# Norm sums of a hybrid encoder layer by 512-column products with constant matrices

## The chip, the core and the metric

The kernel runs on one core of a Trainium2 chip. TensorE (PE) multiplies, VectorE (DVE) and ScalarE (ACT) work elementwise, GpSimd (POOL) fills a few constants, and SyncE (SP) issues the DMAs. Each engine has its own queue of instructions. The metric is the time of one execution on the device, in microseconds; smaller is better.

## The reference, cut to what matters

One layer of a streaming encoder over 256 tokens, width 2048. A modulated norm feeds one input projection; three token mixers (stick-breaking attention, retention, differential attention) work on its columns; their results are gated, merged and projected; a gated MLP with a short convolution follows. The change touches three norms inside the mixers:

```python
def rms_norm(x, g):
    y = x * rsqrt(mean(x * x, axis=-1) + EPS)
    return y * g

# differential attention: 4 heads, each with 2 maps of 64 columns
dq = rope(rms_norm(d_q.reshape(B, S, 4, 2, 64), diff_qn))
dk = rope(rms_norm(d_k.reshape(B, S, 4, 2, 64), diff_kn))
y_diff = differential_attention(dq, dk, d_v, lam)            # heads of 128
y_diff = rms_norm(y_diff, diff_on) * (1.0 - lam_init)

# retention: 4 heads of 256 columns
mu = mean(y, axis=-1); var = mean((y - mu) ** 2, axis=-1)
y_ret = (y - mu) * rsqrt(var + EPS) * g + b                  # then * silu(r_g)
```

## The kernel before, in words

Activations lie with the feature on the partition and the token in the column: `P` = 128 partitions, `S` = 256 tokens. Weights stream from memory in chunks of 128x1024 floats (`raw`). Each chunk is split in two: ACT casts it to a shorter format (`hi`, line 145), DVE subtracts that from the raw one (`lo`, line 118), and PE takes `hi` against a 512-column pair and `lo` against 256 columns (line 349); eight such pairs make one chunk's work. There are 7 buffers for `raw`, 6 for `hi` and 4 for `lo`, so DVE can be at most four chunks ahead of PE. Between chunks DVE also folds the modulation weights (`raw<-raw,c_b`, line 121, one 128x1024 pass each; "modulation pass" below).

The mixers are written as jobs that lie between the units of the gate and branch products: `unit_T` does one unit (four chunks for a gate, one or more for a branch), the list `order` runs through 24 of them, and `jobs` says which job comes before which unit. A scheduler then orders each engine's instructions from priorities and its own estimate of the times, so a job's instructions end up among the products of neighbouring units.

A norm of the mixers is made so: ACT squares, PE sums over partitions with the squares as weights and a column of ones (or `blk`, two columns for the two halves) as the moving operand (`rstd_rows`, line 237). That gives the sum with the token on the partition, 1 to 32 columns wide. DVE makes 1/rms of it by an integer first guess and three Newton steps on these few columns (`small`). To use it, it must go back to token-in-column on all partitions: a column is broadcast to 128 and transposed by PE with `ident` (`spread`, line 253). `diff_prep` does it for q and k of the differential heads at once (for k through a 256-column copy, line 608; the q part stays a per-token scale `qsc`), `diff_pair` for two heads' results, `ret_pair` for two retention heads (`ret_mid` makes their products, lines 706 and 707, copies at 709 and squares at 711). In `diff_head` PE transposes the probabilities at line 645 after DVE has made them. `ret_out` finishes the retention heads: for each head DVE takes a 512-column product with `sum_a`, two with `prm` and two that make the `x` tiles.

ACT's queue also holds ACT_TABLE_LOADs, seven before the change; one of them stands ahead of the first gate's Tanh (line 760).

## Time and profile before

| what | value |
|---|---|
| median of 3 runs | 1528.62 us (1525.99 to 1530.25) |
| profiled execution | 1530.01 us |
| span of its instructions | 1528.2 us |
| PE busy | 1516.9 us (99%) |
| DVE busy | 1251.1 us (82%) |
| ACT busy | 803.0 us (53%) |
| granted clock of PE, mean | 0.999 |
| chain that ended last | PE 91%, DVE 5%, DMA 2%, ACT 1% |

The first row is the metric. The span runs from the first to the last instruction of one profiled execution, and 1.8 us of its time lie outside. Busy shares are of the whole span; matmuls overlap, so a busy PE isn't PE at its peak. The chain is followed back from the last instruction, at each step to what released it.

### The profile page before, as it was taken

How to read it: one execution, taken by the hardware profiler on the slowest of the kernel's cores; microseconds unless marked ns; L12 is line 12 of the kernel's file. 1: busy time of each engine (PE TensorE's matmuls, PEld its weight loads, DVE VectorE, ACT ScalarE, POOL GpSimd, SP SyncE). 2: the span in 40 equal slices, each digit the busy share in tenths (PEclk: the TensorE clock that was granted, in tenths of full speed). 3: DMA queues.
4: the chain of work that ended last, by engine and by line, in shares of the span. 5: the costliest groups of instructions: out<-in, count | busy, mean ns of one | idle time of the engine just before them, and what ended most of it. 6: DMA issues, size and time to landing. Idle time of an engine off the chain costs nothing.

```text
span 1528.2 us, 24447 instructions
## 1 busy us (share of the span) xinstructions
PE 1516.9 (99%) x9228; PEld 1347.0 (88%) x9228; DVE 1251.1 (82%) x2062; ACT 803.0 (53%) x1202; POOL 1.6 (0%) x10
## 2 busy tenths in 40 slices
PE   8999999999999999999999999999999999999999
PEld 7899898988889998888899888888888888888888
DVE  6899889789989899988989877656777776677765
ACT  7534335455654455455557656544565543455541
POOL 0000000000000000000000000000000000000000
PEclk9999999999999999999999999999999999999999
DMA  9988896668799859898966777776777776666672
GB/s 353 327 345 342 308 333 232 198 204 290 257 310 319 328 197 355 310 316 309 321 203 217 234 215 230 226 230 219 226 230 219 224 231 190 187 189 187 187 210 78
DMA packets 108374, 385.38 MB, mean 252 GB/s; under 512 B 12384, under 2 KB 14048, under 8 KB 108256
## 3 DMA queue, kind: packets, MB, share of 16 engines
q1 hardware_dynamic: 108112, 383.75, 76.1%
q8 instruction: 72, 1.18, 0.3%
q14 instruction: 46, 0.38, 0.1%
q10 hardware_dynamic: 144, 0.08, 0.0%
HBM read 379.58 MB, written 2.10 MB: 250 GB/s over the span
## 4 chain that ended last, share of the span: by engine, by line
PE 91%; DVE 5%; DMA 2%; ACT 1%; issue 1%; SPq 0%; ACTq 0%; DVEq 0%
PE acc L349 46%; PE mps L349 26%; PE acc L419 2%; PE acc L418 2%; PE acc L417 2%; DVE lo L118 2%; DVE raw L121 1%; PE acc L431 1%; PE acc L430 1%; PE acc L429 1%; PE mps L417 1%; PE mps L419 1%; PE mps L418 1%; DMA raw<-in_ada 1%; PE mps L430 1%
## 5 line engine op out<-in xcount | busy, mean ns | idle before, releaser
L145 ACT CAST hi<-raw 128x1024 fp32r<-128x1024 f32 x520 | 543.3, 1051 | 436.1 <-PE acc L349 139.0
L118 DVE TENSOR_TENSOR lo<-raw,hi 128x1024 fp32r<-128x1024 f32 x520 | 632.8, 1221 | 145.6 <-PE acc L349 62.6
L349 PE MATMUL acc<-h,hi 128*128 128x512 f32 (+1 forms) x1116 | 392.4, 393 | 0.0
L349 PE MATMUL acc<-h,lo 128*128 128x256 f32 x1104 | 299.4, 281 | 0.0
L121 DVE SCALAR_TENSOR_TENSOR raw<-raw,c_b 128x1024 f32<-128x1024 f32 x192 | 232.0, 1221 | 39.9 <-DMA raw<-in_ada 39.5
L349 PEld LDWEIGHTS acc<-h,hi 128*128 128x128 f32 x1116 | 207.4, 189 | 40.9
L349 PE MATMUL acc<-b,hi 128*128 128x512 f32 x640 | 230.6, 394 | 0.0
L349 PE MATMUL mps<-b,hi 128*128 128x512 f32 x640 | 230.0, 394 | 0.0
L349 PEld LDWEIGHTS acc<-h,lo 128*128 128x128 f32 x1104 | 209.1, 189 | 7.1 <-issue 1.3
L349 PE MATMUL acc<-b,lo 128*128 128x256 f32 x640 | 173.1, 281 | 0.0
L349 PE MATMUL mps<-b,lo 128*128 128x256 f32 x640 | 173.0, 281 | 0.0
L349 PEld LDWEIGHTS acc<-b,hi 128*128 128x128 f32 x640 | 118.9, 188 | 25.0
L349 PEld LDWEIGHTS mps<-b,hi 128*128 128x128 f32 x640 | 118.7, 188 | 25.0
L349 PE MATMUL mps<-h,hi 128*128 128x512 f32 (+1 forms) x380 | 131.7, 387 | 0.0
L349 PEld LDWEIGHTS mps<-b,lo 128*128 128x128 f32 x640 | 120.6, 188 | 3.3
L349 PEld LDWEIGHTS acc<-b,lo 128*128 128x128 f32 x640 | 120.6, 188 | 3.3
L349 PE MATMUL mps<-h,lo 128*128 128x256 f32 x368 | 99.1, 280 | 0.0
L349 PE MATMUL acc<-a,hi 128*128 128x512 f32 (+1 forms) x320 | 91.7, 349 | 0.0
L417 PE MATMUL acc<-h,hi 128*128 128x256 f32 x304 | 83.6, 281 | 1.8 <-ACT h L311 1.8
L418 PE MATMUL acc<-h,hi 128*128 128x256 f32 x304 | 84.8, 281 | 0.0
L419 PE MATMUL acc<-h,lo 128*128 128x256 f32 x304 | 84.2, 283 | 0.3 <-DVE lo L118 0.2
L121 DVE SCALAR_TENSOR_TENSOR tmp<-ftmp,prm,tmp 128x255 f32<-128x255 f32 (+1 forms) x160 | 76.6, 479 | 7.5 <-ACT tmp L883 7.5
(254 smaller groups left out, 2259.9 us busy)
## 6 DMA issues: line engine op xcount, KB each, us to landing
raw<-in_ada SPq DMA_DIRECT2D x192, 512.0 KB, 5.2
raw<-in_wu SPq DMA_DIRECT2D x176, 512.0 KB, 4.3
raw<-in_wg SPq DMA_DIRECT2D x96, 512.0 KB, 4.9
raw<-in_wd SPq DMA_DIRECT2D x88, 512.0 KB, 4.1
raw<-in_w0b SPq DMA_DIRECT2D x32, 512.0 KB, 5.7
raw<-in_w0c SPq DMA_DIRECT2D x32, 512.0 KB, 6.1
raw<-in_w0a SPq DMA_DIRECT2D x32, 512.0 KB, 5.6
raw<-in_wb SPq DMA_DIRECT2D x32, 512.0 KB, 5.4
```

The costliest lines, as they stand in the source:

```text
L118: V.tensor_tensor(out, a, b, op=op)
L121: return V.scalar_tensor_tensor(out, a, s, b, op0=op0, op1=op1, **kw)
L145: return r, hi, SC.copy(hi, r)
L349: PE.matmul(*x, start=first and k == 0, stop=last and k == len(m) - 1)
L417: PE.matmul(dst, wh, hT[kt][:, 0:S], start=(kt == k0 and g % 2 == 0), stop=False)
L418: PE.matmul(dst, wh, hT[kt][:, S:2 * S], start=False, stop=False)
L419: PE.matmul(dst, wl, hT[kt][:, 0:S], start=False, stop=(kt == k1 and g % 2 == 1))
L429: PE.matmul(dst, hh, wh, start=(kt == k0), stop=False)
L430: PE.matmul(dst, hl, wh, start=False, stop=False)
L431: PE.matmul(dst, hh, wl, start=False, stop=(kt == k1))
```

## The change

k of the differential heads, their results and the retention heads get their 1/rms from a new function, `rstd_wide`. PE takes a constant matrix of ones as weights (or `halves`, two 64x64 blocks of ones) and the squares as the moving operand, so that every partition gets the sum with the token in the column. On 512 columns (two heads, or one tile of k) ACT takes logarithm, a scaled copy and exponential, and DVE three steps. The transposes, the broadcasts and the 256-column copies go; q keeps `rstd_rows`, now 16 columns wide.

```diff
-    def spread(cols):
...
+    def rstd_wide(mask, xs_, scale):
+        ss = mps()
+        n = 512 // len(xs_)
+        for k, x in enumerate(xs_):
+            PE.matmul(ss[:, k * n:(k + 1) * n], mask, x, start=True, stop=True)
+        r, v, q = wk(), wk(), wk()
+        SC.activation(r, ss, AF.Ln, bias=eps, scale=scale)
+        SC.activation(r, r, AF.Exp, scale=-0.5)
+        SC.activation(v, ss, AF.Identity, bias=eps, scale=scale)
+        stt(q, v, -0.5, r)
+        tt(q, q, r, ALU.mult)
+        stt(r, q, 1.5, r, op0=ALU.add)
+        return r
...
+    halves = keep.tile([P, P], F32, name="halves")
+    nc.gpsimd.memset(halves, 0.0)
+    for j in range(0, P, 64):
+        nc.gpsimd.memset(halves[j:j + 64, j:j + 64], 1.0)
...
     def diff_prep():
...
-            jobs += [[sq[:, 0:S]], [sq[:, S:2 * S]]]
+            if len(jobs) < 4:
+                jobs += [[sq[:, 0:S]], [sq[:, S:2 * S]]]
+            else:
+                ks.append(sq)
         y = rstd_rows(jobs, blk, 1.0 / 64.0)
         ts_(qsc, y[:, 0:16], 0.125)
+        rk = [rstd_wide(halves, [sq], 1.0 / 64.0) for sq in ks]
...
-            for j in range(2 if k >= 2 else 0):
-                o = 4 * (2 * k + j)
-                e = tmp()
-                V.tensor_copy(e.rearrange("p (a b) -> p a b", b=64),
-                              y[:, o:o + 4].unsqueeze(2).to_broadcast([P, 4, 64]))
-                r = spread([e[:, 0:P], e[:, P:S]])
-                tt(x[:, j * S:(j + 1) * S], x[:, j * S:(j + 1) * S], r, ALU.mult)
+            if k >= 2:
+                tt(x, x, rk[k - 2], ALU.mult)
...
     def diff_pair(h):
...
-        c = rstd_rows(jobs, ones[:, 0:1], 1.0 / 128.0)
+        r = rstd_wide(ones, jobs, 1.0 / 128.0)
         for k, yn in enumerate(yns):
-            r = spread([c[:, 2 * k + b:2 * k + b + 1].to_broadcast([P, P]) for b in range(2)])
-            stt(yn, yn, lamc[:, 1:2], r)
+            stt(yn, yn, lamc[:, 1:2], r[:, k * S:(k + 1) * S])
...
     def ret_pair(h0):
-        jobs = [ret_mid(h0), ret_mid(h0 + 1)]
-        c = rstd_rows(jobs, ones[:, 0:1], 1.0 / 256.0)
+        both_r = rstd_wide(ones, [ret_mid(h0), ret_mid(h0 + 1)], 1.0 / 256.0)
         for k in range(2):
...
-            r = spread([c[:, 2 * k + b:2 * k + b + 1].to_broadcast([P, P]) for b in range(2)])
+            r = both_r[:, k * S:(k + 1) * S]
```

Three places show how the instructions move. The first is ACT's queue at the retention heads. Before, the copies and squares of two heads (lines 709, 711), two casts, and the next two heads:

```order
L709 COPY a_5744<-mps_5739 128x512
L711 ACTIVATE a_5746<-mps_5739 128x512
L709 COPY a_5754<-mps_5749 128x512
L711 ACTIVATE a_5756<-mps_5749 128x512
L145 CAST hi_6015<-raw_6013 128x1024
L145 CAST hi_6040<-raw_6038 128x1024
L709 COPY a_5794<-mps_5789 128x512
L711 ACTIVATE a_5796<-mps_5789 128x512
L709 COPY a_5804<-mps_5799 128x512
L711 ACTIVATE a_5806<-mps_5799 128x512
```

Now (the lines of the copies and squares are 720 and 722; 257, 259 and 258 are logarithm, scaled copy and exponential):

```order
L722 ACTIVATE a_5724<-mps_5717 128x512
L257 ACT_TABLE_LOAD
L257 ACTIVATE a_5730<-mps_5727,eps 128x512
L259 ACTIVATE a_5731<-mps_5727,eps 128x512
L258 ACT_TABLE_LOAD
L258 ACTIVATE a_5730<-a_5730 128x512
L720 COPY a_5748<-mps_5743 128x512
L722 ACTIVATE a_5750<-mps_5743 128x512
L720 COPY a_5758<-mps_5753 128x512
L722 ACTIVATE a_5760<-mps_5753 128x512
L145 CAST hi_5955<-raw_5953 128x1024
L145 CAST hi_5980<-raw_5978 128x1024
```

The five instructions of a pair, two of them table loads, stand ahead of the next two heads' copies and of both casts. The same five, for the second pair, follow these casts. The same two loads stand in each of the six calls of `rstd_wide`, twelve in all.

The second place is DVE's queue from the modulation passes after the retention products on. Before, the few-column steps (`small`) stand among passes and splits:

```order
L118 TENSOR_TENSOR a_5756<-a_5756 128x256
L127 TENSOR_SCALAR small_5764<-mps_5759 128x4
L121 SCALAR_TENSOR_TENSOR raw_6044,part<-raw_6044,c_b 128x1024
L125 TENSOR_SCALAR small_5765<-small_5764 128x4
L118 TENSOR_TENSOR lo_5954<-raw_5950,hi_5952 128x1024
L127 TENSOR_SCALAR small_5765<-small_5765 128x4
L118 TENSOR_TENSOR small_5766<-small_5765 128x4
```

Now:

```order
L121 SCALAR_TENSOR_TENSOR raw_5984,part<-raw_5984,c_b 128x1024
L121 SCALAR_TENSOR_TENSOR a_5732<-a_5731,a_5730 128x512
L118 TENSOR_TENSOR lo_5894<-raw_5890,hi_5892 128x1024
L118 TENSOR_TENSOR a_5732<-a_5732,a_5730 128x512
L118 TENSOR_TENSOR a_5750<-a_5750 128x256
L121 SCALAR_TENSOR_TENSOR a_5730<-a_5732,a_5730 128x512
L118 TENSOR_TENSOR a_5760<-a_5760 128x256
L121 SCALAR_TENSOR_TENSOR a_5712<-a_5712,prm,a_5730 128x256 x2
L121 SCALAR_TENSOR_TENSOR a_5722<-a_5722,prm,a_5730 128x256 x2
L118 TENSOR_TENSOR lo_5935<-raw_5931,hi_5933 128x1024
L121 SCALAR_TENSOR_TENSOR a_5768<-a_5767,a_5766 128x512
L118 TENSOR_TENSOR lo_5957<-raw_5953,hi_5955 128x1024
```

The second row reads `a_5730`, which is ACT's exponential of the first pair, and stands ahead of a split `lo` of the weights; the last row but one reads that of the second pair, again with splits behind it.

The third place is DVE's queue at the end of `ret_out`. Before, up to the two splits there:

```order
L118 TENSOR_TENSOR ftmp_6089<-acc_5989,ftmp_6089 128x256
L121 SCALAR_TENSOR_TENSOR x_6159<-a_6156,x_6159 128x256
L121 SCALAR_TENSOR_TENSOR a_6166<-a_5804,prm,a_6166 128x256 x2
L118 TENSOR_TENSOR ftmp_6094<-acc_5990,ftmp_6094 128x256
L118 TENSOR_TENSOR lo_6182<-raw_6178,hi_6180 128x1024
L121 SCALAR_TENSOR_TENSOR ftmp_6130<-gate_5938,acc_6098 128x256
L121 SCALAR_TENSOR_TENSOR x_6169<-a_6166,x_6169 128x256
L118 TENSOR_TENSOR b_4773<-b_4773,ftmp_6130 128x256
L121 SCALAR_TENSOR_TENSOR ftmp_6133<-gate_5943,acc_6099 128x256
```

Now:

```order
L118 TENSOR_TENSOR ftmp_6034<-acc_5930,ftmp_6034 128x256
L121 SCALAR_TENSOR_TENSOR x_6099<-a_6096,x_6099 128x256 x2
L121 SCALAR_TENSOR_TENSOR ftmp_6070<-gate_5878,acc_6038 128x256
L121 SCALAR_TENSOR_TENSOR a_6106<-a_5758,prm,a_6106 128x256
L118 TENSOR_TENSOR b_4741<-b_4741,ftmp_6070 128x256
L121 SCALAR_TENSOR_TENSOR a_6106<-a_5758,prm,a_6106 128x256
L121 SCALAR_TENSOR_TENSOR ftmp_6073<-gate_5883,acc_6039 128x256
L121 SCALAR_TENSOR_TENSOR x_6109<-a_6106,x_6109 128x256
L118 TENSOR_TENSOR b_4741<-b_4741,ftmp_6073 128x256
L121 SCALAR_TENSOR_TENSOR x_6109<-a_6106,x_6109 128x256
L118 TENSOR_TENSOR lo_6122<-raw_6118,hi_6120 128x1024
```

`lo_6122` is the split that was `lo_6182`. Two gate products (`ftmp<-gate`), two sums (`b`) and two `x` steps that stood behind it stand ahead of it now. Between the split before it (`lo_6104` before, `lo_6044` now) and this one lie now 26 instructions: 4 of 512 columns, 8 with `prm`, 8 of `x`, 2 of `ftmp<-acc`, 2 gate products and 2 sums.

## Rows read from the trace of the kernel before

**Rows 1.** Page, part 1: engine, busy us, share of the span, instructions.

```profile
PE 1516.9 (99%) x9228; PEld 1347.0 (88%) x9228; DVE 1251.1 (82%) x2062; ACT 803.0 (53%) x1202; POOL 1.6 (0%) x10
```

**Rows 2.** Busy by stretch: from:to us, length, engines' busy (instructions), granted clock, DMA.

```profile
316.80:320.30 3.50, 3.50 (x33) 3.46 (x32) 1.42 (x4) 3.23 (x6) 0.00 (x0) 1.00 1.01 394
321.80:325.00 3.20, 3.20 (x12) 2.71 (x11) 3.20 (x7) 0.53 (x1) 0.00 (x0) 0.50 0.25 22
340.00:410.00 70.00, 68.91 (x407) 58.72 (x406) 66.27 (x150) 43.37 (x91) 0.00 (x0) 1.00 0.76 259
...
517.00:557.00 40.00, 39.92 (x258) 35.99 (x257) 36.05 (x90) 22.02 (x39) 0.00 (x0) 1.00 0.57 186
```

**Rows 3.** Timeline of PE at diff_prep: start us, length us, instruction, xcount.

```profile
316.85 3.63 PE L237 MATMUL mps<-x,a 128*128 128x2 f32 x32
320.34 0.49 PE L349 MATMUL acc<-h,hi 128*128 128x512 f32 x1
...
335.47 1.04 PE L253 MATMUL mps<-x,tmp 128*128 128x128 f32 x8
336.27 0.48 PE L349 MATMUL acc<-a,lo 128*128 128x256 f32 x2
```

**Rows 4.** Timeline of PE at the retention heads.

```profile
522.85 0.48 PE L349 MATMUL acc<-h,hi 128*128 128x512 f32 x1
...
524.22 0.50 PE L237 MATMUL mps<-ones,a 128*128 128x1 f32 x4
524.58 0.37 PE L349 MATMUL acc<-h,lo 128*128 128x256 f32 x1
...
532.09 0.62 PE L253 MATMUL mps<-x,small 128*128 128x128 f32 x4
532.54 0.60 PE L706 MATMUL mps<-a,a 128*128 128x256 f32 x2
532.98 0.39 PE L707 MATMUL mps<-a,a 128*128 128x128 f32 x2
```

**Rows 5.** What PE waited for, 300 to 560 us: us in total, times, longest.

```profile
PE mps L645 <- DVE a L121: 0.9, 2, 0.7
```

**Rows 6.** Timeline of PE: transposes of the second differential head's probabilities, brackets: idle before.

```profile
366.21 0.30 PE L645 MATMUL mps<-x,a 128*128 128x128 f32 x1 [0.25 <-DVE a L121]
```

**Rows 7.** Timeline of ACT: a table load, and a 512-column square of retention.

```profile
317.44 1.28 ACT L760 ACT_TABLE_LOAD   x1
318.73 0.72 ACT L760 ACTIVATE gate<-ftmp 128x256 f32<-128x256 f32 x2
...
523.62 0.60 ACT L711 ACTIVATE a<-mps 128x512 f32<-128x512 f32 x1
```

**Rows 8.** Timeline of DVE: two waits at diff_prep.

```profile
320.51 0.19 DVE L127 TENSOR_SCALAR small<-mps 128x32 f32<-128x32 f32 x1 [2.30 <-PE mps L237]
...
327.84 1.22 DVE L118 TENSOR_TENSOR lo<-raw,hi 128x1024 fp32r<-128x1024 f32 x1 [1.14 <-issue]
```

**Rows 9.** Timeline of DVE in ret_out; the last row is PE's first use.

```profile
545.27 1.23 DVE L118 TENSOR_TENSOR lo<-raw,hi 128x1024 fp32r<-128x1024 f32 x1 [0.22 <-PE acc L349]
...
552.43 0.68 DVE L121 SCALAR_TENSOR_TENSOR a<-a,b 128x512 f32<-128x512 f32 x1
553.04 0.42 DVE L121 SCALAR_TENSOR_TENSOR x<-a,x 128x256 fp32r<-128x256 f32 x1
...
554.04 0.87 DVE L121 SCALAR_TENSOR_TENSOR a<-a,prm,a 128x256 f32<-128x256 f32 x2
554.83 0.42 DVE L118 TENSOR_TENSOR ftmp<-acc,ftmp 128x256 f32<-128x256 f32 x1
555.16 1.22 DVE L118 TENSOR_TENSOR lo<-raw,hi 128x1024 fp32r<-128x1024 f32 x1
556.30 0.41 DVE L121 SCALAR_TENSOR_TENSOR ftmp<-gate,acc 128x256 f32<-128x256 f32 x1
...
556.94 0.28 PE L349 MATMUL acc<-h,lo 128*128 128x256 f32 x1
```

More of the change, by code (lines that the diff above doesn't have):

```diff
@@ L247, in rstd_rows @@
         return y
-    def spread(cols):
-        ps = mps()[:, :S]
-        for b in range(2):
-            PE.transpose(ps[:, b * P:(b + 1) * P], cols[b], ident)
-        return ps
+    def rstd_wide(mask, xs_, scale):
[11 more added lines that the diff above has]
+        return r
     sq = []
@@ L594, in diff_prep @@
     def diff_prep():
-        jobs = []
+        jobs, ks = [], []
         for x in qd + kd:
@@ L659, in diff_pair @@
             SC.activation(sq, yn, AF.Square)
-            jobs.append([sq])
-        c = rstd_rows(jobs, ones[:, 0:1], 1.0 / 128.0)
+            jobs.append(sq)
+        r = rstd_wide(ones, jobs, 1.0 / 128.0)
         for k, yn in enumerate(yns):
-            r = spread([c[:, 2 * k + b:2 * k + b + 1].to_broadcast([P, P]) for b in range(2)])
-            stt(yn, yn, lamc[:, 1:2], r)
+            stt(yn, yn, lamc[:, 1:2], r[:, k * S:(k + 1) * S])
             o = slot(F32R)
@@ L713, in ret_mid @@
         tt(sq[:, 0:S], sq[:, 0:S], sq[:, S:2 * S], ALU.add)
-        return [sq[:, 0:S]]
+        return sq[:, 0:S]
     def ret_pair(h0):
-        jobs = [ret_mid(h0), ret_mid(h0 + 1)]
-        c = rstd_rows(jobs, ones[:, 0:1], 1.0 / 256.0)
+        both_r = rstd_wide(ones, [ret_mid(h0), ret_mid(h0 + 1)], 1.0 / 256.0)
         for k in range(2):
```

## The prediction, as it was made before the run

> **What bounds the kernel now.** I read the busy shares first, then the waits, then the timelines of the stretch that the change touches. PE is busy for 99% of the span [rows 1]; in 300 to 560 us the view of waits names DVE for it twice, 0.9 us in all, ahead of the transposes at line 645 [rows 5]. So a microsecond of PE's own work counts in full, as long as DVE and ACT stay ahead. How far ahead they are differs by place. At the differential heads (340 to 410) DVE is busy for 66.27 of 70 us [rows 2] and PE already waits for it at the second head's transposes, at 366.21 [rows 6]: there DVE sets the pace. At the retention heads (517 to 557) PE hardly waits, but the cover is thin at one place: the split that DVE starts at 555.16 ends at 556.38, and PE takes it at 556.94 [rows 9]. The reader is to see 0.56 us of slack there. ACT is half idle [rows 1]; it matters by when its results come, not by its load.
>
> **PE's work.** At diff_prep 16 two-column sums stand from 316.85 to 320.34 (two records each, hence x32), 3.49 us [rows 3]; the half for k goes, 1.75. The eight transposes go, 335.47 to 336.27, 0.80. Two 512-column products come. A 256-column one takes 532.54 to 532.98, two records, 0.44 [rows 4], so I take 0.87 for twice the columns; the bound below is 0.44, if a wider one cost no more. Sum: -1.75 - 0.80 + 1.74 = -0.8. Each of the four pairs of heads loses four one-column sums, two times 0.36 (524.22 to 524.58), and four transposes, 0.45 (532.09 to 532.54), and gets two 256-column products, 0.86 [rows 4]: -0.3, four times -1.2.
>
> **PE's clock.** From 321.80 to 325.00 the granted clock is 0.50, that is 1.2 instead of 2.4 GHz; it is 1.00 from 316.80 to 320.30, which are the two-column sums [rows 2, 3], and 0.999 over the span. 3.20 us at half cost 1.6 us of work. With half of these sums and two full-width products behind them I expect no fall here: -1.6. The bound is 0, if the fall stays.
>
> **The differential heads: nothing is left of it.** Up to the first head's probabilities DVE loses four 256-column copies and four 256-column multiplies, and two modulation passes move behind it; it gets six 512-column steps and two 512-column multiplies. At 0.61 for 512 columns, 0.33 for 256 and 1.14 for a 1024-column pass (by the starts in [rows 9]) that is 8 x 0.61 - 8 x 0.33 - 2 x 1.14 = about 0. Its idle time changes little too. Before, it waits 2.30 us for the sums and 1.14 later [rows 8]. Now the sums come 1.75 earlier, but DVE's first wide step of the second k tile needs the second exponential: from the gates at about 320.2, ACT has load, Ln, Identity, load, Exp (1.28 + 0.5 + 0.5 + 1.28 + 0.6 = 4.2 by [rows 7], where the next 512-column instruction starts some 0.5 after one of 0.6), a cast (1.05), and 4.2 again: 329.7. By its own queue DVE gets there at 328.1, so it waits 1.6. So DVE finishes the first head's probabilities about when it does now, and PE, 0.8 + 1.6 us earlier, waits some 2 us for them at line 645, where its two waits now are 0.7 and 0.25 [rows 5, 6]. One pass comes back before the second head, and one before the fourth, 1.14 each, against some 1.2 saved in the pair's steps. I take 0 for all up to 410 us, between -3.5 (all PE savings stay) and +2 (DVE later by its new wait, which nothing then hides). Only the second pair's -0.3 lies behind the last wait.
>
> **The retention heads: where a new wait comes.** PE saves 2 x 0.3. The chain that is new runs through ACT. The second head's square ends at 524.22 [rows 7]. A load fits in until 525.5. The second sum product ends at about 525.7 (by PE's order behind 522.85: two pairs of 0.35, a product 0.43, one head's products 1.30, a product 0.43). Then Ln 0.5, Identity 0.6, load 1.28, Exp 0.6: 528.9. DVE is at the step that needs it by about 526 and waits; behind that step stand the splits. From 528.9 DVE does, by the order, three wide steps, two splits, two 256-column sums and four `y` multiplies (0.40): 1.83 + 2.28 + 0.66 + 1.60 = 6.4, so 535.3. ACT meanwhile has two copies and two squares, four times 0.5, two casts, 2.1, load, Ln, Identity, load, Exp, 4.3: 537.2. DVE waits again, 1.9. From 537.2 come three wide steps, four splits, a modulation pass, four `y` multiplies, two sums `ftmp`, two gate products and two sums `b`: 1.83 + 4.56 + 1.14 + 1.60 + 0.66 + 1.32 = 11.1, so 548.3. Then the block of 26 instructions without a split: 4 x 0.61 + 8 x 0.40 + 14 x 0.33 = 10.3, so 558.6, and the split ends at 559.8. Before, it ended at 556.38: the block was 8.7 us long (from the end of the split begun at 545.27 to 555.16) [rows 9], since two gate products, two sums and two `x` steps stood behind it. PE, 0.6 earlier, wants it at 556.3. So PE stands still for 3.5 us. From below I bound it by 0: DVE's added work alone, without its two waits (4.7 us together), would end in time. From above by 6, if ACT comes 1 us later at each of the two.
>
> **What that standstill does to the clock.** The only stretch of some 3.5 us with hardly any work for PE was followed by 3.2 us at 0.50 [rows 2, 3]; PE's waits now are all under 1 us and followed by none. A standstill of 3.5 us is nearer to the first: +1.6, with 0 as the other end.
>
> **No price:** the three fills of `halves` on POOL stand ahead of the last ones of a constant that PE needs first at 5 us, and are a fraction of a microsecond each. SP's loads of the swapped halves move by a few places, under splits that end 4 us and more before their use at the differential heads.
>
> **The sum.** Against the profiled execution: 1530.01 + 0 - 0.3 - 0.6 + 3.5 + 1.6 = 1534.2, that is +4.2. The profile was 1.4 above the median, inside the spread of the three runs, so I put the +4.2 on the median: 1532.8.
>
> **The rivals.**
> - The standstill comes, but the clock doesn't fall: 1528.62 - 0.9 + 3.5 = 1531.2. For it: no row shows a true standstill of this length. Against it: PE does even less than in the sums.
> - The savings stay: DVE and ACT hold their lead, the waits for the exponentials are idle time that DVE has anyway (40 - 36.05 = 3.95 us between 517 and 557 [rows 2]). Then -0.8 - 1.2 - 1.6 = -3.6: 1525.0. For it: DVE's added work alone fits. Against it: the block without a split got longer by 1.6 us where 0.56 were spare.
> - On the other side, slower beyond what can be told from no change: the preparation's new wait (DVE for the second exponential, 329.7) isn't made up by the sums that come earlier. From about 1.7 us on, PE stands over 3.5 us at the first head's transposes, and the clock falls there as well. 2 + 1.6 on top of the forecast: 1536.4.
> - ACT's load costs as much again in emptying the engine: each call's Exp 2.6 us later, so the second one of retention 5.2 later, and so the split: 1538.0. The Trainium skill says so (ScalarE: Activation LUTs, What ACT_TABLE_LOAD costs): 1283 ns for a load and some 1380 ns of drain at every switch of sets. By that rule the forecast would be 1538.0; the trace speaks against it, since the load takes 1.28 us and the next activation starts as it ends, 318.73 [rows 7].
>
> **How the numbers follow.** A measurement of this kernel can tell 0.3% from no change, 4.6 us: 1524.0 to 1533.2. Forecast (standstill and clock) 0.38, no fall of the clock 0.24, savings stay 0.18, preparation late as well 0.15, slow loads 0.05. The forecast's own time is uncertain by 2 us, so some 0.4 of it lies above 1533.2, with a little of the second case and nearly all of the last two: slower 0.37. Of the third case a quarter lies below 1524.0: faster 0.05. Within 0.3%: 0.58. For 8 times in 10 the range goes from 1525.0, the middle of the third case, to 1537.0, past the fourth; it leaves out half of the third (0.09), the last (0.05) and the upper part of the fourth.
>
> **What would show it right or wrong.** Right: twelve more table loads on ACT; in DVE's rows idle time of 2 to 3 us and of about 2 us ahead of wide steps, released by ACT's line 258; one wait of PE for `lo` of 2 to 5 us at about 556, and a granted clock of 0.50 behind it; no 0.50 at about 322; waits of PE at line 645 grown to some 2 us. Wrong: PE without a wait at 556, or with the clock at 0.50 after the sums still; an end more than 4 us away from the forecast with these waits present would mean that a cost lies elsewhere.

## The result, and the profile after

The changed kernel is slower: 1538.61 us (median of 6 runs, 1537.32 to 1540.13) against 1529.53 for the kernel before on the same chip. The ratio is 1.0064, with an interval from 1.0054 to 1.0073. Its profiled execution took 1537.67 us, span 1535.8; against the profiled execution of before that is +7.7 us. The profiled executions lie apart by less than the medians (+9.1 us), within the spread of the runs; what follows explains the 7.7. The forecast was 1532.8 with a range up to 1537.0: the sign of the sum held, its size didn't.

The page's first part, busy time by engine, answers to [rows 1]:

```profile
PE 1518.7 (99%) x9176; PEld 1345.3 (88%) x9176; DVE 1253.9 (82%) x2026; ACT 828.5 (54%) x1232; POOL 1.9 (0%) x13
```

PE's busy time grew by 1.8 us although it has less to do, DVE's by 2.8 and ACT's by 25.5. None of that explains 7.7 us. PE's waits and the clock do. This is the view of PE's waits from 335 to 600 us (line and tile, what it waited for: total, times, longest):

```profile
PE acc L362 <- DVE lo L118: 3.6, 2, 3.2
PE acc L362 <- DVE ftmp L118: 2.4, 3, 1.0
PE mps L657 <- DVE a L121: 2.1, 1, 2.1
PE mps L661 <- ACT a L659: 0.8, 2, 0.5
```

Before, DVE was named twice there with 0.9 us in all [rows 5]. Line 657 is the old line 645, the transposes of the first head's probabilities. Where the big waits lie is seen in PE's timeline (start, duration, instruction, and in brackets the idle time before it and who ended it):

```profile
350.56 0.33 PE L657 MATMUL mps<-x,a 128*128 128x128 f32 x1 [2.09 <-DVE a L121]
...
463.90 0.50 PE L362 MATMUL acc<-h,hi 128*128 128x512 f32 x1 [0.91 <-DVE ftmp L118]
...
563.06 0.58 PE L362 MATMUL acc<-h,lo 128*128 128x256 f32 x1 [3.15 <-DVE lo L118]
```

And the clock, in the view of stretches (from:to and length, then busy time of PE, its weight loads, DVE, ACT and POOL, the granted clock, the DMA share and GB/s); it answers to [rows 2]:

```profile
320.00:324.00 4.00, 4.00 (x25) 3.52 (x24) 3.68 (x9) 3.96 (x6) 0.00 (x0) 1.00 0.41 102
348.00:352.00 4.00, 1.91 (x11) 1.36 (x10) 4.00 (x11) 1.14 (x3) 0.00 (x0) 0.93 0.91 310
352.00:356.00 4.00, 3.76 (x19) 2.86 (x18) 2.60 (x6) 3.02 (x8) 0.00 (x0) 0.64 1.02 334
560.00:564.00 4.00, 0.94 (x3) 0.85 (x4) 4.00 (x8) 0.67 (x2) 0.00 (x0) 0.88 0.00 0
564.00:568.00 4.00, 4.00 (x19) 3.50 (x18) 4.00 (x7) 1.06 (x1) 0.00 (x0) 0.69 0.95 262
```

The fall at 322 is gone, as forecast. Two others have come, one behind the standstill at 350 and one behind that at 563.

A ledger shows nearly the whole 7.7 us. It is worked out from the two timelines of PE: for the same piece of weights, the time at which PE takes it after the change minus the time before. The places are in the time of the changed kernel.

| up to | what lies there | after minus before, us | step |
|---|---|---|---|
| 316 | start-up loads, not touched by the change | -1.1 | |
| 340 | narrow sums gone, clock doesn't fall | -3.2 | -2.1 |
| 357 | first head: standstill 2.1, clock 0.64 behind it, a copy of ACT late | +1.7 | +4.8 |
| 420 | the other heads | +1.1 | -0.6 |
| 465 | DVE behind a modulation pass that waits for its load | +2.3 | +1.2 |
| 559 | retention up to the late split | +2.6 | +0.3 |
| 563 | standstill | +6.0 | +3.4 |
| 570 | clock behind it | +7.5 | +1.5 |

### The profile page after: what moved, and what is told of

The parts are those of the page before. It is cut to its first block, busy times and chain, and to the rows that moved or that the text cites. A ratio compares the mean times of both kernels' runs of the same rounds, so it can differ in the third digit from the quotient of the medians.

```text
span 1535.8 us, 24312 instructions
## 1 busy us (share of the span) xinstructions
PE 1518.7 (99%) x9176; PEld 1345.3 (88%) x9176; DVE 1253.9 (82%) x2026; ACT 828.5 (54%) x1232; POOL 1.9 (0%) x13
## 4 chain that ended last, share of the span: by engine, by line
PE 88%; DVE 5%; DMA 3%; ACT 2%; issue 1%; SPq 0%; DVEq 0%; ACTq 0%
PE acc L362 44%; PE mps L362 26%; PE acc L432 2%; PE acc L431 2%; PE acc L430 2%; DVE lo L118 1%; DVE raw L121 1%; PE acc L442 1%; PE acc L444 1%; PE acc L443 1%; PE mps L430 1%; ACT hi L145 1%; PE mps L432 1%; DMA raw<-in_wg 1%; PE mps L431 1%
```

## The experiments

Two theories stood at the start. The first is that of the prediction, widened by the ledger: PE stands because DVE waits for an exponential that comes late, since every call of `rstd_wide` makes ACT load two tables. The rival: the loads matter little, DVE simply has too much work between splits, or has it in a bad order.

### One part alone: e1_k_only, e2_diff_only, e3_ret_only

Each kernel has the wide sums in one place and the old ones in the other two. Shown is what e1 puts back into the changed kernel, for the heads' results and for retention; e2 and e3 are made the same way.

```diff
+    def spread(cols):
...
-        r = rstd_wide(ones, jobs, 1.0 / 128.0)
+        c = rstd_rows(jobs, ones[:, 0:1], 1.0 / 128.0)
...
-        both_r = rstd_wide(ones, [ret_mid(h0), ret_mid(h0 + 1)], 1.0 / 256.0)
+        c = rstd_rows(jobs, ones[:, 0:1], 1.0 / 256.0)
```

> Only diff_prep has the wide sums (for k); the pairs of differential and retention heads keep their few-column sums. My theory (the cost at the first differential head comes from diff_prep's second exponential, which DVE waits for at about 329 us): PE stands about 2 us at the first head's transposes at 350, the clock falls behind it, no fall at 322; in the span -2.1 for the work saved, +4.3 up to 420, so about +2 against the kernel before, in the median 1530.5 to 1533. Rival (the cost at the differential heads belongs to the pairs' own calls): no standstill at 350, and 1527 to 1528.

> Only the pairs of differential heads have the wide sums. My theory: nothing happens at 350, the fall of the clock at 322 stays as before, DVE gets some 1.2 us of wide steps less few-column steps, PE saves 2 x 0.3: 1528 to 1530.5. Rival (the pairs' calls, with two table loads each among the heads' exponentials, make the heads late): PE waits of 2 us and more between 350 and 410, and 1531 to 1534.

> Only the retention heads have the wide sums. My theory: the chain through ACT alone makes one split 3.5 us late in ret_out, PE stands 3 to 3.5 us there and the clock falls behind it for 1.5: +5 against the kernel before, 1533.5 to 1535.5. Rival (the standstill needs the lateness that DVE brings from the differential heads, or the modulation passes that moved): under 1 us of standstill, no fall of the clock, 1528 to 1530.5.

| kernel | median, us | to before (same chip), us | ratio |
|---|---|---|---|
| e1_k_only | 1533.94 | +4.9 | 1.0031 [1.0020, 1.0043] |
| e2_diff_only | 1536.68 | +7.6 | 1.0045 [1.0030, 1.0061] |
| e3_ret_only | 1531.27 | +2.2 | 1.0016 [1.0007, 1.0024] |

None of the three times lies in the range of the author's theory. They sum to +14.7, but the whole change costs 9.1. So these kernels don't measure parts of the change, and neither theory's numbers for them can be weighed against these. The reason stands in their traces: the scheduler makes the order of all engines anew behind each edit. In e2, where retention is as before, PE waits 2.0 us for a split at 566, where neither the kernel before nor the changed one waits. In e3 the wait at retention is 1.0 instead of 3.2. What e1 does show is that the wide sums of the preparation are enough for a standstill at the first head (loads, steps and order together), by two of the four rows of its waits of PE from 300 to 600 us:

```profile
PE mps L668 <- ACT a L666: 2.1, 2, 1.1
PE mps L664 <- DVE a L121: 1.8, 1, 1.8
```

### Fewer table loads in a new order: e4_one_set

All three parts are changed, and before each logarithm one set is loaded that has logarithm and exponential both.

```diff
+        table = SC.preload_act_table_set("natural_log_exp_and_others")
+        before(squared[-1], table)
+        if mask is halves:
+            before(nxt[-1][1], table)
...
-        SC.activation(r, ss, AF.Ln, bias=eps, scale=scale)
+        ln = SC.activation(r, ss, AF.Ln, bias=eps, scale=scale)
+        before(table, ln)
```

> The changed kernel with one table load ahead of each logarithm, of a set that has the exponential too; the load of the gates' set comes behind. Each exponential of the pairs comes 1.28 us earlier, retention's second one 2.6. My theory (DVE waits for the chain on ACT, and PE for DVE): DVE's two waits at the retention heads fall from 2.7 and 2.1 to about 1.4 and under 1, the standstill at 561 from 3.2 to about 1, without a fall of the clock; at diff_prep one load less on the chain too, so some 1.3 less at 350: 5 to 7 us under the changed kernel, 1531 to 1534. Rival (DVE's added work and its new order alone make the splits late): the standstills stay within 0.5 us, and 1537 to 1539.

Measured: 1528.46 us, -0.6 to before, ratio 0.9994 [0.9985, 1.0003], below the ranges of both theories. That is 10 us less than the changed kernel, more than the loads can account for by their own time (two fewer, 1.28 us each), and the order is again a new one: at retention the standstill is 1.2 instead of 3.2, and the one at the first head is now behind ACT's copy of the transposes. The two longest of PE's waits from 300 to 600 us:

```profile
PE mps L668 <- ACT a L666: 1.7, 1, 1.7
PE acc L369 <- DVE lo L118: 1.2, 1, 1.2
```

### The order held: h0_held, h1_no_loads, h2_no_wait, h3_split_first, h4_one_set_held

To change one thing at a time, the order of the changed kernel's instructions was recorded for each engine, and each experiment is given that order by dependencies that only order (`ORDER` is the record).

```diff
+def hold_order(tc):
+    order = json.loads(zlib.decompress(base64.b85decode(ORDER)))
+    here = {i.name: i for i in tc.nc.cur_bb.bb.instructions}
+    for row in order.values():
+        row = [here[f"I-{n}"] for n in row if f"I-{n}" in here]
+        for first, then in zip(row, row[1:]):
+            tc.add_manual_dep(then, first.name, mybir.DependencyInfo(
+                mybir.DependencyClass.NoSync, mybir.DependencyReason.DATA), reason="held order")
```

h0 is the control, with nothing else changed.

> The changed kernel with its order held and nothing else changed: the same instructions in the same order. 1537.5 to 1540, with the standstills of 2.1 and 3.2 us at 350 and 561. If the fall of the clock follows from the standstill alone it comes at both again; if not, one may be missing and the time some 1.5 us less.

h1 takes the loads away: logarithm and exponential become scaled copies, so the norms are left out.

```diff
-        SC.activation(r, ss, AF.Ln, bias=eps, scale=scale)
-        SC.activation(r, r, AF.Exp, scale=-0.5)
+        SC.activation(r, ss, AF.Identity, bias=eps, scale=0.0)
+        SC.activation(r, r, AF.Identity, scale=-0.5)
```

> The changed kernel with every engine's order of instructions held as it is, but logarithm and exponential of the wide sums are replaced by plain scaled copies, so that none of the twelve table loads is left (the norms are not computed). DVE does the same work in the same order. Theory A (the loads make the exponentials late, DVE waits for them, PE for DVE): the waits of 2.5, 2.7 and 2.1 us on DVE go, the standstills at 350 and 561 and the falls of the clock behind them go, 1526 to 1530. Theory B (DVE's 512-column steps and their places ahead of the splits are enough): standstills within 0.7 us of the changed kernel's, 1536 to 1539.

h2 keeps the loads and takes the wait away: DVE's three steps read a constant, so the norms are left out here too.

```diff
-        stt(q, v, -0.5, r)
-        tt(q, q, r, ALU.mult)
-        stt(r, q, 1.5, r, op0=ALU.add)
-        return r
+        stt(q, c_b[:, 0:512], -0.5, c_b[:, 0:512])
+        tt(q, q, c_b[:, 0:512], ALU.mult)
+        stt(q, q, 1.5, c_b[:, 0:512], op0=ALU.add)
+        return q
```

> The changed kernel in its held order, with all its work on ACT, loads too, but DVE's three steps read a constant tile in place of what ACT made (the norms are not used). Theory A: as with no loads, 1526 to 1530, since only the waiting for the exponentials costs. Theory B: 1536 to 1539. Theory C (the loads cost by making ACT's casts of the weights late, not by the exponentials): 1534 to 1538, with splits that wait for casts.

h3 moves one split (`lo_6122`, the late one of retention) ten places forward in DVE's order; these are the rows of DVE's order that differ.

```diff
 L118 TENSOR_TENSOR ftmp_6034<-acc_5930,ftmp_6034 128x256
+L118 TENSOR_TENSOR lo_6122<-raw_6118,hi_6120 128x1024
 L121 SCALAR_TENSOR_TENSOR x_6099<-a_6096,x_6099 128x256 x2
...
 L121 SCALAR_TENSOR_TENSOR x_6109<-a_6106,x_6109 128x256
-L118 TENSOR_TENSOR lo_6122<-raw_6118,hi_6120 128x1024
 L121 SCALAR_TENSOR_TENSOR raw_6124,part<-raw_6124,c_b 128x1024
```

> The changed kernel in its held order but for one instruction: on DVE, the split that PE stands still for at 561 is taken ten places forward, ahead of gate products, sums and the last steps of ret_out. Theory A: the standstill is that split's alone, 3.2 us and 1.5 for the clock, so 1533 to 1535. Rival (what now stands behind the split is wanted as soon: PE waits for the evacuations or the products of the gates instead): 1536.5 to 1539.

h4 has five loads of the set with both functions (the second k tile needs none of its own), in the held order. With four that other activations then need for their own sets these are nine added loads instead of twelve.

```diff
-        SC.activation(r, ss, AF.Ln, bias=eps, scale=scale)
+        lns.append(SC.activation(r, ss, AF.Ln, bias=eps, scale=scale))
...
+    hold_order(tc, {ln.ins.name: SC.preload_act_table_set("natural_log_exp_and_others")
+                    for ln in lns[:1] + lns[2:]})
```

> The changed kernel in its held order, with five loads of the set that has both functions in place of the twelve, and four loads of the gates' set further behind. Against the earlier variant with one set, whose order the scheduler chose anew, this tells the loads from the order. Theory A (the gain of 10 us came from the shorter chain): 1528 to 1531. Rival (it came from the other order): 1535 to 1539.

| kernel | median, us | to before, us | ratio | PE's wait at the first head's transposes (line 657) | a few products on, for ACT's copy of them (line 661) | at the late split |
|---|---|---|---|---|---|---|
| h0_held | 1537.37 | +7.7 | 1.0051 [1.0037, 1.0065] | 2.2 | 0.5 | 3.1 |
| h1_no_loads | 1531.90 | +2.1 | 1.0014 [1.0005, 1.0023] | none | 0.9 | 2.3 |
| h2_no_wait | 1535.67 | +5.9 | 1.0038 [1.0025, 1.0050] | 2.2 | 0.7 | 3.1 |
| h3_split_first | 1536.86 | +7.0 | 1.0052 [1.0039, 1.0066] | 1.9 | none | 2.8, one split later |
| h4_one_set_held | 1533.22 | +3.4 | 1.0020 [1.0011, 1.0029] | none | 1.7 | 3.0 |

**h0** gives the changed kernel's time again, so holding the order costs nothing that can be seen. h1 and h4 lie between the ranges of their two theories, h2 in that of theory C, and h3 in that of its rival, though PE waits for something else than the rival named.

**The differential heads: the loads are the cause of most of the loss.** Without them (h1), and with fewer (h4), the wait at line 657 is gone. PE doesn't go free, though: in h4 it stands 1.74 us a few products on, for ACT's copy:

```profile
350.92 0.70 PE L661 MATMUL mps<-a,a 128*128 128x256 f32 x2 [1.74 <-ACT a L659]
```

The ledger, made for these kernels in the same way, says what is won. From 316 to 420 us the changed kernel has +2.2 against before, h0 +1.7, h2 +0.6, h4 -0.3 and h1 -1.3. So the loads are worth some 3 us there, of which h2 wins about 1 by taking away the wait for the exponentials. That wait is not the whole cause: h2 has none and PE still stands 2.2 us at line 657. The two longest of h2's waits of PE from 300 to 600 us:

```profile
PE acc L362 <- DVE lo L118: 3.1, 1, 3.1
PE mps L657 <- DVE a L121: 2.2, 1, 2.2
```

DVE's timeline in h2 shows what took the wait's place:

```profile
331.45 1.23 DVE L118 TENSOR_TENSOR lo<-raw,hi 128x1024 fp32r<-128x1024 f32 x1 [0.21 <-ACT hi L145]
...
334.55 0.76 DVE L118 TENSOR_TENSOR ftmp<-acc,ftmp 128x256 f32<-128x256 f32 x2 [1.28 <-ACT ftmp L399]
```

Casts and the copies that evacuate products (line 399) stand behind the loads in ACT's queue. They come late as well, and DVE, which works in order, waits for them if it doesn't wait for the exponential.

**The retention heads: the loads are not the cause of the standstill.** At the late split it is 2.3 us without loads (h1), 3.1 without waits (h2) and 3.0 with fewer loads (h4), against 3.1 in h0; at most 0.8 of it goes with the loads. h3 then shows that it isn't a matter of that one split either: PE gets it in time and stands 2.8 us for the next, which DVE starts 5.74 us behind it. DVE's splits and PE's wait in h3:

```profile
558.10 1.22 DVE L118 TENSOR_TENSOR lo<-raw,hi 128x1024 fp32r<-128x1024 f32 x1
...
563.84 1.23 DVE L118 TENSOR_TENSOR lo<-raw,hi 128x1024 fp32r<-128x1024 f32 x1
```

```profile
565.12 0.39 PE L362 MATMUL acc<-h,lo 128*128 128x256 f32 x1 [2.81 <-DVE lo L118]
```

A sum comes within 0.4 us of PE's wait in every one of these kernels. A chunk keeps PE busy for 2.8 us; so the standstill is the time between the starts of two splits, less the lead that the first of them has on PE (from its end to PE's use of it), less 2.8.

| kernel | between the starts | lead | sum | PE's wait |
|---|---|---|---|---|
| before | 9.89 | 7.63 | -0.5 | none |
| after | 11.72 | 5.43 | 3.5 | 3.2 |
| h1_no_loads | 11.66 | 6.19 | 2.7 | 2.3 |
| h2_no_wait | 11.74 | 5.47 | 3.5 | 3.1 |
| h4_one_set_held | 11.56 | 5.43 | 3.3 | 3.0 |

After the change the two splits that make the 11.72 are these, in DVE's timeline, and what lies between them is the block of correction, gate and `x` steps:

```profile
550.07 1.23 DVE L118 TENSOR_TENSOR lo<-raw,hi 128x1024 fp32r<-128x1024 f32 x1
...
561.79 1.22 DVE L118 TENSOR_TENSOR lo<-raw,hi 128x1024 fp32r<-128x1024 f32 x1
```

Before, they stood at 545.27 and 555.16 [rows 9]. So 1.8 us of the 4.0 (from -0.5 to 3.5) are the longer block and 2.2 the smaller lead. h2 shows that the lead is not lost to the waits for exponentials: it has none and the lead is the same.

### Where the lead goes: h5_no_ret_steps, h6_no_wait_5lo

h5 takes away DVE's own added work at retention, the six correction steps (order held). h6 is h2 with a fifth buffer for `lo`, since DVE in h2 waits 2.21 us at 531.22 for PE to free one. First h5's edit, ahead of DVE's three steps (`next_id` only keeps the names as they were):

```diff
+        if scale == 1.0 / 256.0:
+            return r if [nc.next_id() for _ in range(3)] else None
```

> The changed kernel in its held order, with all table loads and all waits, but without DVE's three 512-column correction steps at the two pairs of retention heads (the exponential is used as it is): 6 x 0.61 = 3.7 us less for DVE between 530 and 545. Theory D, which the runs before have left (DVE's own work between two splits is too much for the lead that it has; its waits for the exponentials only take the place of waits for buffers): the lead of the last split ahead of ret_out's block grows from 5.4 to 7.5 us and more, the standstill at 561 falls from 3.2 to under 1, no fall of the clock there, 1533 to 1535.5. Theory A for this place (the waits for the exponentials): the standstill stays above 2, 1537 to 1539.

And h6's, on top of h2:

```diff
-    wlo = ctx.enter_context(tc.tile_pool(name="wlo", bufs=4))
+    wlo = ctx.enter_context(tc.tile_pool(name="wlo", bufs=5))
```

> The held order without waits for the exponentials (the norms are not used), and with five buffers for the splits in place of four. Theory D: what DVE no longer waits for the exponentials it waited, with four buffers, for PE to free one (2.2 us at 531); with a fifth it keeps these 2.2 us, so the lead ahead of ret_out's block is about 7.5 instead of 5.5 us, the standstill there 1 instead of 3.1, and the time 2 to 4 us under that with four. Rival (the lead is set by something else, such as the casts or the transfers): lead and standstill as with four, time within 1 us.

Measured: h5 1534.33 us (+5.0, ratio 1.0035 [1.0022, 1.0049]), its standstill at the split 2.4 (starts 11.54 apart, lead 6.06). h6 1534.58 us (+5.3, 1.0028 [1.0018, 1.0038]), standstill 3.1 (11.73 and 5.46). h5's time lies in theory D's range, but its standstill isn't under 1 as that theory has it; in h6 lead and standstill are as with four buffers, as the rival has it. So the six steps are worth some 0.7 us of the standstill, and a fifth buffer nothing: in h6 DVE's wait has moved to an evacuation copy, in its timeline:

```profile
538.18 0.42 DVE L118 TENSOR_TENSOR ftmp<-acc,ftmp 128x256 f32<-128x256 f32 x1 [1.80 <-ACT ftmp L399]
```

That copy follows PE's own product. If DVE gets ahead, it is held there, so a lead won earlier is lost at this place; the split behind it has a lead of 6.5 us in after, h0, h2, h4 and h6 alike. That this is why the lead ahead of the block is the same is argued from these rows, and for h2 and h6 alone: in after, h0 and h4 DVE doesn't wait at this copy but for exponentials (2.71 and 2.08 in after), and no kernel was run that takes the copy away. Why the lead ends at 6.5 in all five stays open.

### Without the correction steps: p1_no_steps, p2_no_steps_held

Both have one set for logarithm and exponential, five loads of it, and leave out the scaled copy and DVE's three steps. p1 has the scheduler's own order, p2 the held one.

```diff
-        SC.activation(v, ss, AF.Identity, bias=eps, scale=scale)
-        stt(q, v, -0.5, r)
-        tt(q, q, r, ALU.mult)
-        stt(r, q, 1.5, r, op0=ALU.add)
```

> A version meant to be used: the wide sums at all places, one load of the set with both functions ahead of each logarithm (one for both tiles of k), and 1/rms taken as the exponential gives it, without the scaled copy on ACT and the three steps on DVE; the scheduler's own order. Theory D and the loads together: 18 x 0.61 = 11 us less for DVE than in the changed kernel, no standstill above 1 us at 350 and 560, so the savings on PE stay: 1525 to 1528. Rival (the gates' loads and the logarithm's still push casts back at the differential heads): 1528 to 1531.

> The same work in the changed kernel's held order, to be set against the held order with one set and with the steps (1533.2, a standstill of 3.0 at 557). Theory D: that standstill falls to under 0.5, the one at 350 stays on ACT's copy (1.7): 1526 to 1529. Rival (the order, with its block of 26 instructions without a split, costs by itself): still 2 us and more at 557, 1530 to 1533.

Measured: p1 1531.06 us (+1.8, ratio 1.0008 [0.9999, 1.0017]) and p2 1530.71 (+1.4, 1.0008 [0.9999, 1.0016]). Leaving out work and loads brings both back to about the time of the kernel before, and no further. p2 did what its rival says; p1 lies just above the ranges of both theories. p2's waits from 300 to 600 us name the two that are left:

```profile
PE acc L359 <- DVE lo L118: 2.3, 1, 2.3
PE mps L658 <- ACT a L656: 2.0, 2, 1.7
```

p1 has neither, and instead a rope step of DVE that waits 2.27 for a load, with PE behind it. Again a new order makes a new wait.

### The order alone: h7_spread

The changed kernel, all its instructions, order held but for one stretch of DVE: the late split and the next three go ahead, gate products, sums, modulation passes and the last `x` steps go between and behind them (ACT's last `x` activations two casts later, to match). The core of the difference in DVE's order:

```diff
 L121 SCALAR_TENSOR_TENSOR a1125_6096<-a1055_5748,prm_111,a1125_6096 128x256 x2
+L118 TENSOR_TENSOR lo1133_6122<-raw1131_6118,hi1132_6120 128x1024
 L118 TENSOR_TENSOR ftmp1113_6034<-acc1094_5930,ftmp1113_6034 128x256
+L121 SCALAR_TENSOR_TENSOR ftmp1119_6070<-gate1081_5878,acc1114_6038 128x256
...
+L118 TENSOR_TENSOR lo1137_6147<-raw1135_6143,hi1136_6145 128x1024
+L121 SCALAR_TENSOR_TENSOR raw1134_6124,part_126<-raw1134_6124,c_b_133 128x1024
+L118 TENSOR_TENSOR lo1141_6172<-raw1139_6168,hi1140_6170 128x1024
 L121 SCALAR_TENSOR_TENSOR x1126_6099<-a1125_6096,x1126_6099 128x256 x2
...
+L118 TENSOR_TENSOR lo1144_6194<-raw1142_6190,hi1143_6192 128x1024
...
-L118 TENSOR_TENSOR lo1133_6122<-raw1131_6118,hi1132_6120 128x1024
...
-L118 TENSOR_TENSOR lo1137_6147<-raw1135_6143,hi1136_6145 128x1024
```

> The changed kernel in its held order, but at the end of ret_out the four splits ahead of and around 561 stand where PE wants them, and the gate products, sums, modulation passes and the last steps of ret_out stand between and behind them (their results are wanted 25 us later); no work is changed, all loads and waits stay. Theory of the order: the standstill at 561 falls under 0.5 us, none over 0.5 comes at the three splits behind it, no fall of the clock there: 4 to 5 us under the changed kernel, 1533 to 1535. Rival (DVE has too much work in the stretch, wherever it stands): the standstill comes back at a later split, as it did when one split was moved, 1536 to 1539.

Measured: 1533.52 us, +3.8 to before, ratio 1.0028 [1.0017, 1.0039]; that is 3.9 less than the control h0. The standstill is gone and none comes at the next three splits (starts 7.66 apart at the first, so its sum is below zero; it has 0.78 us to spare, the next ones 0.34, 0.87 and 1.85). The view of stretches shows PE full and the clock whole where the standstill and the fall were:

```profile
556.00:560.00 4.00, 4.00 (x32) 3.91 (x31) 3.96 (x9) 1.83 (x7) 0.00 (x0) 1.00 0.00 0
560.00:564.00 4.00, 4.00 (x24) 3.50 (x24) 3.97 (x7) 1.43 (x2) 0.00 (x0) 1.00 0.63 159
```

Nothing was taken out, no load and no step. So the retention standstill is a matter of what stands ahead of the splits in DVE's order. What h7 still costs lies elsewhere: PE waits 1.8 us at the first head, with a fall of the clock behind it, 1.69 at 464.22 and 1.04 at 546.90, the last two for sums of DVE.

### Both put right: b1_best

p2, with h7's order at retention, and at the first head ACT's copy of the transposes (line 656 here) three places earlier, ahead of a gate activation, an evacuation copy and a cast. These are the rows of ACT's order there:

```diff
 L145 CAST hi721_4116<-raw720_4114 128x1024
+L656 COPY a623_3717<-mps622_3713 128x384
 L767 ACTIVATE gate694_3994<-ftmp695_3995 128x256
 L396 COPY ftmp705_4032<-acc698_4004 128x256
 L145 CAST hi730_4150<-raw729_4148 128x1024
-L656 COPY a623_3717<-mps622_3713 128x384
```

> A version meant to be used: five loads of the set with both functions, no correction steps, the spread order of DVE at the end of ret_out, and on ACT the copy of the first differential head's transposes taken ahead of a cast and two other instructions. Against the same without the last two (1530.7, with a standstill of 2.3 and a fall of the clock at 556 and 1.7 at 351): both standstills under 0.5, so 2.3 + 1.4 + 1.2 less: 1525 to 1527. Rival (DVE meets PE again a little later at each place): 1528 to 1531.

Measured: 1526.54 us (median of 11 runs, 1525.67 to 1527.42), -3.2 to before, ratio 0.9979 [0.9971, 0.9988]. This version is faster than both kernels: 10.8 us below the control h0, which ran beside it. The standstill at retention is gone; at the first head 0.8 and 0.5 us are left, somewhat more than expected. Its waits of PE from 300 to 600 us, and its busy times:

```profile
PE mps L658 <- ACT a L656: 0.8, 1, 0.8
PE mps L654 <- DVE a L121: 0.5, 1, 0.5
```

```profile
PE 1514.7 (99%) x9176; PEld 1342.5 (88%) x9176; DVE 1245.1 (82%) x2008; ACT 822.5 (54%) x1223; POOL 1.9 (0%) x13
```

What the change could bring is about what the prediction's third case (savings stay, -3.6) had worked out from PE's rows: -3.2 was measured with the same 9176 instructions on PE. It comes only where DVE and ACT keep ahead.

## Why the prediction was wrong, point by point

**PE's own work and the fall at 322: right.** The prediction had -0.8 and -1.6 for the preparation. The ledger has -2.1 up to 340 us, and the clock is 1.00 from 320 to 324.

**The differential heads, taken as 0: this step failed.** From 316 to 420 us the ledger has +2.2, a little above the upper bound given. Two terms were wrong.
- The wait for the second exponential was put at 1.6 us. In DVE's timeline after the change it is 2.53; the first one is 0.32, and both are released by line 258 as foreseen:

```profile
323.76 0.69 DVE L121 SCALAR_TENSOR_TENSOR a<-a,a 128x512 f32<-128x512 f32 x1 [0.32 <-ACT a L258]
...
329.22 0.69 DVE L121 SCALAR_TENSOR_TENSOR a<-a,a 128x512 f32<-128x512 f32 x1 [2.53 <-ACT a L258]
```

- "PE waits some 2 us at line 645" was right (2.09), but the prediction set that against the time PE had gained and gave it no price of its own in the clock. The granted clock fell to 0.64 behind it. That is the prediction's fourth case, preparation late and the clock falling there as well, at 1536.4; the forecast's +4.2 had no room for it. The fall alone isn't the miss: h0 has none there and still +1.7 in the same stretch. And the reason given was too narrow: only the exponential was followed through ACT's queue, not the casts and copies behind the loads (h2).

**462 us: not foreseen.** DVE gets to a modulation pass earlier than its load and waits, as it does near there in the kernel before (1.77 and 1.29 us), but now PE waits 0.9 for the sum behind it:

```profile
462.28 1.23 DVE L121 SCALAR_TENSOR_TENSOR raw<-raw,c_b 128x1024 f32<-128x1024 f32 x1 [2.08 <-DMA raw<-in_ada]
```

The prediction gave moved passes DVE's time only and not the time of their loads. The ledger's +1.2 lies here. h1, without table loads, loses 1.2 here too, and h4 nothing; what sets it wasn't tested alone.

**The retention heads: the size was right, the cause wrong.** Forecast were 3.5 us of standstill and 1.6 of clock; the ledger has 3.4 and 1.5. With the cause wrong, that is luck: the split ends at 563.01 and PE is ready for it at 559.91, 3.2 and 3.6 us later than worked out. The waits for exponentials were put at 2.9 and 1.9 us and are 2.71 and 2.08:

```profile
531.64 0.69 DVE L121 SCALAR_TENSOR_TENSOR a<-a,a 128x512 f32<-128x512 f32 x1 [2.71 <-ACT a L258]
...
540.13 0.69 DVE L121 SCALAR_TENSOR_TENSOR a<-a,a 128x512 f32<-128x512 f32 x1 [2.08 <-ACT a L258]
```

But the step "DVE's added work alone, without its two waits, would end in time" failed. Without these waits the standstill is as long (h2, 3.1 us), without loads 2.3 (h1), and without the added steps 2.4 (h5). For this standstill the waits are not a cause that adds up: had DVE not waited there, it would have waited for a buffer or an evacuation (h2: 2.21 us for PE, 0.66 for ACT's copy). What decides is what DVE does between that point and the split, and its order (h7). The block's growth, +1.6 forecast and +1.8 measured, was the part of the working that was sound. The PE savings of 0.6 forecast at retention don't show, the ledger has +0.3 there, and here the lateness does cost: PE waits for a sum of DVE ahead of the standstill,

```profile
546.61 0.50 PE L362 MATMUL acc<-h,hi 128*128 128x512 f32 x1 [1.04 <-DVE ftmp L118]
```

which it doesn't without the waits (h2), with fewer loads (h4) or without the added steps (h5). From 520 to 556 us these three win 1.2 to 1.3 against before; the prediction priced the chain through ACT at the late split only.

**The start.** The ledger's -1.1 up to 316 us, where nothing was changed, was luck as well: it hides as much of what the forecast missed. What it missed is the +2.2 at the heads, the +1.2 at 462 and the 0.9 of savings behind the heads. The end is 5.8 us from the forecast with the waits present, which by the prediction's own sign means that a cost lies elsewhere, and it does.

**ACT's load.** The rival by which a load costs as much again in emptying the engine fell. After the change, at the first retention call (ACT's timeline), the next activation starts as the load ends, 529.68 + 1.28 = 530.96:

```profile
528.98 0.68 ACT L259 ACTIVATE a<-mps,eps 128x512 f32<-128x512 f32 x1
529.68 1.28 ACT L258 ACT_TABLE_LOAD   x1
530.97 0.63 ACT L258 ACTIVATE a<-a 128x512 f32<-128x512 f32 x1
```

The Trainium skill (ScalarE: Activation LUTs, What ACT_TABLE_LOAD costs) gives 1283 ns for a load, which agrees with these rows, and a further drain of some 1380 ns at a switch, which they don't show. The Trainium skill (the same page, Rules for kernel authors) advises one set that has both exponential and logarithm for calls such as these; h4 bears that out with 4.3 us less than its control h0, each against the kernel before beside it, in the same order.

## What to carry to other kernels

Where an engine works in order, an added wait isn't simply added to the end: ask which wait comes next if it is taken away, and what else stands behind the slow instruction in its queue. A late split is found by three numbers from the rows, the time between the starts of two splits, the lead of the first and the consumer's time for one chunk, and moving work behind the split can be worth more than removing work. Parts of a change are compared in a held order, with a control, or the effect of a new order is taken for the part's (here three parts summed to 14.7 us where the whole cost 9.1).

## What the runs showed of the hardware that was not expected

**The clock falls behind some standstills and not behind others, with the same instructions.** h0 has the changed kernel's instructions in the changed kernel's order. Behind its wait of 2.2 us at the first head the clock stays at 1.00, where the changed kernel had 0.64 behind 2.1; behind the one of 3.1 at retention it falls as there:

```profile
352.00:356.00 4.00, 2.18 (x14) 1.95 (x14) 4.00 (x12) 2.37 (x4) 0.00 (x0) 1.00 0.96 342
564.00:568.00 4.00, 3.00 (x10) 2.61 (x11) 4.00 (x5) 0.00 (x0) 0.00 (x0) 0.52 0.47 131
568.00:572.00 4.00, 4.00 (x17) 3.48 (x16) 4.00 (x7) 1.04 (x1) 0.00 (x0) 0.63 0.96 303
```

And h4, with a wait of 3.0 us in 556 to 560, has no fall:

```profile
556.00:560.00 4.00, 2.86 (x17) 2.55 (x18) 4.00 (x5) 0.00 (x0) 0.00 (x0) 1.00 0.37 122
560.00:564.00 4.00, 4.00 (x24) 3.49 (x24) 4.00 (x7) 1.05 (x1) 0.00 (x0) 1.00 0.95 308
```

Over the profiled executions of the kernels here, standstills of 1.7 to 2.2 us at the first head were followed by a fall in 6 of 11, those of 2.3 to 3.2 us at retention in 5 of 9. The fall at retention cost 1.5 us in the ledger after the change; h0's lasts twice as long, and its profiled execution, at 1540.70 us, is 3.3 over its median. What decides it is open; for a single profile it means that 1.5 us and more at each such place can come or not. The Trainium skill (TensorE: Matmul & The Clock Gate, Part 1) says that the window in which the chip looks at PE's activity runs freely and isn't tied to the kernel's start. That would fit an effect that comes and goes, but no run here shows it.

**A fall followed the two-column sums, too, where PE was never idle.** 32 records of them were followed by 3.2 us at 0.50 in the kernel before; e2 and e3, which keep all 32, have a fall there as well (in e2 it sets in before they end), and no kernel with 16 has it.
